# Dilated attention and convolution in an encoder layer: queries copied into the second pattern's order, loads moved ahead, the last heads regrouped

## The chip, the cores and the metric

The kernel runs on one core of a Trainium2 chip. The metric is the device time of one execution in microseconds. The engines are TensorE (PE; its weight loads are listed apart as PEld), VectorE (DVE), ScalarE (ACT), GpSimd (POOL) and SyncE (SP), which issues most of the DMAs. Each engine works through its own queue in order; where one needs another's result it waits on a semaphore.

## The reference

One layer of a bidirectional encoder over 2048 positions of width 1024, float32. An RMSNorm and one projection give queries, keys and values (8 heads of 64) and the two inputs of a gated convolution (512 channels). Then come attention and convolution side by side, an output projection, a cross-attention to 256 memory rows, an MLP of width 4096 with a squared ReLU, and a last RMSNorm. What the change touches is the attention over three dilated patterns, merged by their log-denominators, and the convolution:

```
DILATED_PATTERNS = ((128, 1), (512, 4), (2048, 16))
for window, d in DILATED_PATTERNS:
    half = window // (2 * d)
    o, lse = banded_attention(to_strided(q, d), to_strided(k, d), to_strided(v, d), half)
    outs.append(from_strided(o, d, B)); lses.append(from_strided(lse, d, B))
w = softmax(stack(lses), axis=0)
o = sum(w[..., None] * stack(outs), axis=0)
...
u = a * sigmoid(g)
u = conv1d_depthwise(u, conv_w, width=31) + conv_b
u = silu(layernorm(u, ln_g, ln_b))
```

Pattern 0 takes neighbouring positions, pattern 1 every fourth, pattern 2 (the far one) every sixteenth; each looks 64 steps to either side.

## The kernel before

Matrices are kept as a high and a low part, and a product is three matmuls (high by high, low by high, high by low; `mm3`, lines 198 to 200). Weights come as tiles `raw` of 512 KB, are split by ACT (high, line 189) and DVE or POOL (low, line 190), and have a few places each.

The positions are handled in four groups of 512. After the projections (0 to about 550 us of the profile) the attention of group 0 runs (`att(0, p2_)`), woven with the rest of the convolution gates (`rest`) and the first convolution's layer norm. Far units for all positions (`att_far`, line 800 and on) are done here, four per head, ahead of that head's near units. Then `post(p)` runs for each group: output projection (`o`), cross-attention (`xs`, `x`), MLP (`up`, `dn`), final norm. While `post(p)` runs, the attention and convolution of group p + 1 are woven in by rates: `weave` advances a side by so many steps per step of the main work. The order in which instructions stand on each engine is then fixed by the framework's scheduler when the program is built. `issue_after` (in `pinned` and `after`) holds some of them behind the last instruction of a named engine.

A near unit (`unit` in `att_units`) handles one head, one pattern and two blocks of 128 queries. It has three parts, taken in turn with those of the next units: scores on PE (`s`, line 948, four matmuls of 128x256: two blocks, each with the high and the low queries as weights), mask and row minimum on DVE (line 751) and the exponential on ACT (752); transposes on PE (758) and a split into `ph` and `pl` (761, 762); the product with the values on PE (`opt`, lines 766 to 768). Two units (g = 0, 1) make a head and pattern. Within a head pattern 1 comes first, then pattern 0. The weights of pattern 0's scores are 128 neighbouring columns of the query tile; those of pattern 1 are every fourth:

```
if pat == 0:
    qs = slice(P * blk, P * blk + P)
    kv = k[:, :, 8 * blk + 12:8 * blk + 28].rearrange("p r (c i) -> p c r i", c=2)
else:
    qs = slice(blk, 512, 4)
    kv = k[:, blk:16:4, 0:64].rearrange("p r (c i) -> p c r i", c=2)
```

Queries and keys are loaded on SP for a pair of heads at a time (`load_keys`): the high part `qh` (two transfers, two buffers), the low part `ql` (one transfer, one of two buffers) and, in groups 1 to 3, the near keys `k` of 512 KB (two buffers). In group 0 the near units use the far keys `k3`. The values of a pair are loaded together at the end of the pair before (`load_v`).

Pattern 1's and the far pattern's outputs go through memory (`oscr`, stored from ACT's queue), to come back in natural order. When a pair is done `combine` loads them (`ld`), forms the weights of the three patterns and adds them up on POOL (lines 868 to 894, `cat`), with small steps on DVE and ACT between, PE transposes the result (`catT`, line 902), and it goes to memory (`cath`, `catl`) for the output projection, which reads the last pair's part last.

The convolution of 512 positions and 128 channels (`conv_unit`) loads its input `cu` and does 31 steps on DVE (lines 210 and 212), then stores; four such units make a group.

POOL does little else after the projections: the power in `newton_rsqrt` (176), and one subtraction per tile in the convolution's norm (268).

Of the kernel before, what the change touches and what calls it, by code (L numbers as in the profile page):

```python
# [47 lines left out]
def hybrid_layer(ctx, tc, A, out):  # L48
# [157 lines left out]
    def conv_unit(c, n, alloc):  # L206
        u = alloc("u", (P, 542), f"cu{c}_{n}")
        dma(u, uscr[c][:, 512 * n:512 * n + 542])
        acc = alloc("acc", (P, 512), f"cacc{c}_{n}")
        DVE.tensor_scalar(acc, u[:, 0:512], cw[:, c, 0:1], gain("conv_b", c), op0=ALU.mult, op1=ALU.add)  # L210
        for t in range(1, CW):
            DVE.scalar_tensor_tensor(acc, u[:, t:t + 512], cw[:, c, t:t + 1], acc, op0=ALU.mult, op1=ALU.add)  # L212
            if t % 4 == 0:
                yield
        dma(cscr[c][:, 512 * n:512 * (n + 1)], acc)
        yield
# [502 lines left out]
    with ExitStack() as st:  # L719
        lbk = pool("lin_k", stack=st)  # L720
        cu = pool("conv0", stack=st)
        conv0 = pinned(conv_units(cu, 0, (0, 1)), "dve")
        weave(islice(steps, 31), (vsc, 0.42), (conv0, 0.5))
        drain(vsc, conv0)
        next(steps)
    with ExitStack() as st:
        lbv = pool("lin_v", stack=st)
        cu = pool("conv0b", stack=st)
        conv0 = pinned(conv_units(cu, 0, (2, 3)), "dve")
# [47 lines left out]
    def load_keys(h, p):  # L777

        k = None
        if p:  # L780
            k = kq.tile([P, 16, 64], F32R, tag="k", name=f"k{p}{h}", bufs=2)
            dma(f(k), f(kscr[:, :, h].rearrange("x d r i -> (x d) r i")[:, :, 32 * p:32 * p + 64]))
# [21 lines left out]
    def att_far(p2_, h, k, vt, q):  # L804
# [105 lines left out]
    def att_units(p, far, then):  # L910
# [4 lines left out]
        vt = {}  # L915

        def load_v(pr):
            es = slice(pr * 2 * VW, (pr + 1) * 2 * VW)
            if far:
                vt[2] = far.tile([P, 16, 2 * VW], F16, tag="v3", name=f"v3_{pr}")  # L920
                dma(vt[2], vtok[256:256 + S, es].rearrange("(i r) e -> i r e", r=16))
            vt[1] = aq.tile([P, 4, 2, 2 * VW], F16, tag="v2", name=f"v2_{p}{pr}")
            for c in range(2):
                src = vtok[512 * (p + c):512 * (p + c) + 512, es].rearrange("(i a b) e -> b a i e", a=4, b=4)
                for b in range(4):
                    dma(vt[1][:, b, c], src[b])
            vt[0] = aq.tile([P, 5, 2 * VW], F16, tag="v1", name=f"v1_{p}{pr}")
            for c in range(5):
                t0 = 256 + 512 * p + P * c - 64
                dma(vt[0][:, c], vtok[t0:t0 + P, es].rearrange("(i r) e -> r i e", r=16))  # L930

        def unit(pr, hh, pat, g, k, q_, os_, opt):
# [3 lines left out]
            for z in range(2):  # L936
# [5 lines left out]
                else:  # L942
                    qs = slice(blk, 512, 4)
# [28 lines left out]
            if g and hh and not pat:  # L972
                then(pr, os_)
                if pr < H // 2 - 1:
                    load_v(pr + 1)

        for pr in range(H // 2):
            if pr == 0:
                load_v(0)
            K = [load_keys(2 * pr + hh, p) for hh in range(2)]  # L980
            o0 = aq.tile([P, 4, 2, ROW], F32, tag="o0", name=f"o0_{p}{pr}", bufs=2)
            o1 = None
            for hh in range(2):
                k, q_ = K[hh]
                if far:
                    h, k = 2 * pr + hh, keys
# [3 lines left out]
                if hh == 0:  # L990
                    o1 = (far if far and pr % 2 else aq).tile([P, 4, 2, ROW], F32, tag="o1", name=f"o1_{p}{pr}")
# [53 lines left out]
    with ExitStack() as st:  # L1045
# [26 lines left out]
        weave(islice(first, 74), (rest, 0.8))  # L1072
# [302 lines left out]
```

## Time and profile before

| | |
|---|---|
| time, three runs | 2935.51, 2942.90, 2942.61 us; median 2942.61 |
| the profiled execution | 2945.54 us, its span 2943.7 us |
| PE busy | 2867.2 us (97%) |
| PEld (weight loads) | 2447.8 us (83%) |
| DVE busy | 1836.3 us (62%) |
| ACT busy | 1188.1 us (40%) |
| POOL busy | 396.8 us (13%) |
| moved by DMA | 434.87 MB |
| mean granted clock | 0.988 |

The span runs from the first to the last instruction; the time is a little longer. A row of the timeline gives start and length in microseconds, engine, line, operation, what is written from what, and in brackets the engine's idle time before it and what ended that. A row of the table by stages gives for each engine the busy time and the number of instructions, then the granted clock, the mean share of the DMA engines and GB/s. A row of a source line gives the number of instructions and the shortest, median and longest duration in ns. A row of waits gives the total, the number of times and the longest.

### The profile page before, as it was taken

To read this page: it belongs to the slowest core of one execution; us is meant where nothing else is said; L and a number is where in the kernel's file an instruction comes from. 1 tells how busy PE (TensorE), PEld (TensorE's weight loads), DVE (VectorE), ACT (ScalarE), POOL (GpSimd) and SP (SyncE) were. 2 spreads that over 40 slices of the span, in tenths; PEclk is the share of its full clock that TensorE was granted. 3 is DMA by queue.
4 is the path that set the end of the run, shared out by engine and by line. 5 is a ranking of instruction groups with operands and counts; after the bars stand their busy time and mean duration, and the time that the engine had idled before them with its cause. 6 is when DMAs were issued, how large, how long until landed. Compare 5 with 4: busy or idle time off the path is not lost.

```text
span 2943.7 us, 42766 instructions
## 1 busy us (share of the span) xinstructions
PE 2867.2 (97%) x16396; PEld 2447.8 (83%) x16396; DVE 1836.3 (62%) x3295; ACT 1188.1 (40%) x2002; POOL 396.8 (13%) x470
## 2 busy tenths in 40 slices
PE   8999999989799999999999999999999999999999
PEld 7878889878598888888888888898888888888888
DVE  5636444555668866576697766677867555544445
ACT  5632211566345333344443334444433344432333
POOL 1346421122100111010020012000110110000000
PEclk9999999999899999999999999999999999999999
DMA  8978844889724544464353445624434355233332
GB/s 265 295 165 212 194 135 134 197 224 253 186 81 137 141 124 125 129 183 163 107 136 122 127 129 167 188 102 130 131 118 122 104 161 170 92 94 100 93 100 72
DMA packets 620804, 434.87 MB, mean 148 GB/s; under 512 B 191333, under 2 KB 549785, under 8 KB 620600
## 3 DMA queue, kind: packets, MB, share of 16 engines
q1 hardware_dynamic: 582168, 414.05, 49.7%
q10 hardware_dynamic: 38432, 18.09, 2.5%
q8 instruction: 129, 2.11, 0.3%
q14 instruction: 75, 0.61, 0.1%
HBM read 340.42 MB, written 91.64 MB: 147 GB/s over the span
## 4 chain that ended last, share of the span: by engine, by line
PE 79%; DVE 3%; DMA 2%; ACT 2%; issue 1%; SPq 1%; POOL 1%; ACTq 0%; POOLq 0%; DVEq 0%
PE up L198 8%; PE dn L198 8%; PE up L200 8%; PE up L199 8%; PE dn L199 8%; PE dn L200 8%; PE s L948 2%; PE x L198 2%; PE xs L198 2%; PE x L200 2%; PE x L199 2%; PE o L198 2%; PE xs L200 2%; PE xs L199 2%; PE o L199 2%; PE o L200 2%
## 5 line engine op out<-in xcount | busy, mean ns | idle before, releaser
L199 PE MATMUL dn<-hhl,whi_d 128*128 128x512 f32 (+1 forms) x1056 | 404.2, 385 | 0.0
L200 PE MATMUL dn<-hhh,wlo_d 128*128 128x512 f32 (+1 forms) x1056 | 403.4, 384 | 0.0
L198 PE MATMUL up<-mh,whi_u 128*128 128x512 f32 x1024 | 402.0, 393 | 0.5 <-DVE rl L1246 0.5
L198 PE MATMUL dn<-hhh,whi_d 128*128 128x512 f32 (+1 forms) x1056 | 400.3, 392 | 1.7 <-DVE h L1264 1.6
L200 PE MATMUL up<-mh,wlo_u 128*128 128x512 f32 x1024 | 399.5, 390 | 0.0
L199 PE MATMUL up<-ml,whi_u 128*128 128x512 f32 x1024 | 398.8, 389 | 0.0
L212 DVE SCALAR_TENSOR_TENSOR cacc<-cu,cw,cacc 128x512 f32<-128x512 f32 x480 | 384.3, 803 | 5.3
L1264 DVE TENSOR_TENSOR h<-h,dn 128x512 f32<-128x512 f32 (+1 forms) x264 | 172.4, 667 | 216.6 <-PE dn L200 215.2
L189 ACT CAST whi_d<-raw_d 128x1024 fp32r<-128x1024 f32 x128 | 134.6, 1051 | 403.8 <-PE up L199 352.0
L189 ACT CAST whi_u<-raw_u 128x1024 fp32r<-128x1024 f32 x128 | 134.6, 1051 | 379.8 <-PE dn L199 322.5
L198 PEld LDWEIGHTS dn<-hhh,whi_d 128*128 128x128 f32 x1056 | 197.5, 188 | 40.9 <-DVE h L1264 5.4
L1246 DVE SCALAR_TENSOR_TENSOR rl<-up,ssumx 128x512 f32<-128x512 f32 x128 | 88.0, 691 | 229.4 <-PE up L200 225.6
L200 PEld LDWEIGHTS dn<-hhh,wlo_d 128*128 128x128 f32 x1056 | 198.5, 188 | 39.2
L199 PEld LDWEIGHTS dn<-hhl,whi_d 128*128 128x128 f32 x1056 | 198.8, 188 | 35.8
L200 PEld LDWEIGHTS up<-mh,wlo_u 128*128 128x128 f32 x1024 | 192.2, 188 | 40.3
L199 PEld LDWEIGHTS up<-ml,whi_u 128*128 128x128 f32 x1024 | 192.4, 188 | 38.2
L198 PEld LDWEIGHTS up<-mh,whi_u 128*128 128x128 f32 x1024 | 192.2, 188 | 38.5 <-DVE rl L1246 0.9
L752 ACT ACTIVATE sm<-sm,o 128x256 f32<-128x256 f32 (+1 forms) x384 | 159.0, 465 | 118.4 <-DVE o L751 109.6
L190 DVE TENSOR_TENSOR wlo_d<-raw_d,whi_d 128x1024 fp32r<-128x1024 f32 x128 | 158.2, 1236 | 24.6 <-ACT whi_d L189 24.6
L190 DVE TENSOR_TENSOR wlo_u<-raw_u,whi_u 128x1024 fp32r<-128x1024 f32 x128 | 158.9, 1242 | 22.3 <-ACT whi_u L189 22.1
L751 DVE CUSTOM_DVE_ANT_0 sm<-s,mask 128x256 f32<-128x256 f32 (+1 forms) x384 | 127.8, 374 | 47.7 <-PE s L948 33.4
L762 DVE TENSOR_TENSOR pl<-pt,ph 128x512 f16<-128x512 f32 x160 | 109.2, 686 | 66.6 <-ACT ph L761 66.6
(386 smaller groups left out, 6521.6 us busy)
## 6 DMA issues: line engine op xcount, KB each, us to landing
raw_u<-in_w_up_dram SPq DMA_DIRECT2D x128, 512.0 KB
raw_d<-in_w_down_dram SPq DMA_DIRECT2D x128, 512.0 KB
raw_o<-in_w_out_dram SPq DMA_DIRECT2D x32, 512.0 KB
raw_a<-ascr SPq DMA_DIRECT2D x32, 512.0 KB
raw_b<-bscr SPq DMA_DIRECT2D x32, 512.0 KB
v<-vtok SPq DMA_DIRECT2D x208, 65.0 KB
k<-kscr SPq DMA_DIRECT2D x24, 512.0 KB
k<-kscr SPq DMA_DIRECT2D x8, 1152.0 KB
```

Source lines behind the costliest of these rows:

```text
L189: ACT.copy(hi, raw)
L190: (lo_eng or DVE).tensor_tensor(lo, raw, f(hi), op=ALU.subtract)
L198: PE.matmul(o, lh, rh, start=first, stop=False)
L199: PE.matmul(o, lh, rl, start=False, stop=False)
L200: last["pe"] = PE.matmul(o, ll, rh, start=False, stop=end)
L212: DVE.scalar_tensor_tensor(acc, u[:, t:t + 512], cw[:, c, t:t + 1], acc, op0=ALU.mult, op1=ALU.add)
L751: last["dve"] = DVE.tensor_tensor_reduce(dst, so, mask[:, 256 * m:256 * m + nk], 1.0, 3e38, ALU.add, ALU.min, mn)
L752: last["act"] = ACT.activation(dst, dst, AF.Exp, bias=mn, scale=-1.0)
L762: DVE.tensor_tensor(pl, pt, ph, op=ALU.subtract)
L948: last["pe"] = PE.matmul(o, q_[x][:, qs], kv, start=x == 0, stop=x == 1)
L1246: last["dve"] = DVE.scalar_tensor_tensor(r, pt, 0.0, rsb, op0=ALU.max, op1=ALU.mult)
L1264: last["dve"] = DVE.tensor_tensor(hs[m][:, sl], hs[m][:, sl], pt, op=ALU.add)
```

## The change

Four things are done.

In the near attention pattern 0 now comes first and pattern 1 second. A new function `turned` copies a head's queries on POOL, high (128x512) and low (64x512), so that each block's every-fourth columns lie side by side; pattern 1's scores read the copy. The copy takes the second of the `qh` buffers and the second of the `ql` buffers, so that loaded queries have one buffer each. Queries and keys of a head are loaded one head ahead, behind the previous head's pattern-0 units, instead of for two heads at a time. Values are loaded in two parts, pattern 0's behind the last pattern-0 unit of a pair, the others behind its last unit.

In group 0 the last two heads (`end`) do the far units of both first, then pattern 1 of both, then pattern 0 of both, with the old reading of the queries; their near keys are loaded apart (`keys_of`) into the places of the far queries.

The convolution's input is loaded by a function of its own: two steps ahead of the first unit, and one unit ahead for the others (not in the two early pools).

The combination waits one step longer before its loads, except for the last pair of group 0, and the rates of three weaves are changed.

```diff
-    def conv_unit(c, n, alloc):
+    def conv_load(c, n, alloc):
         u = alloc("u", (P, 542), f"cu{c}_{n}")
         dma(u, uscr[c][:, 512 * n:512 * n + 542])
+        return u
+
+    def conv_unit(c, n, alloc, u):
...
-    def conv_units(pl, n, cs=range(4)):
-        for c in cs:
-            yield from conv_unit(c, n, lambda role, shape, name: pl.tile(list(shape), F32, tag=role, name=name, bufs=2))
+    def conv_units(pl, n, cs=(0, 1, 2, 3), ahead=True):
...
+        u = conv_load(cs[0], n, alloc)
+        yield
+        yield
+        for i, c in enumerate(cs):
+            nxt = conv_load(cs[i + 1], n, alloc) if ahead and i + 1 < len(cs) else None
+            yield from conv_unit(c, n, alloc, u)
+            u = nxt or (conv_load(cs[i + 1], n, alloc) if i + 1 < len(cs) else None)
...
-    def load_keys(h, p):
+    def load_keys(h, p, slot=0):
...
-        ql = qlow[h % 2]
+        ql = qlow[slot]
...
+    def turned(h, p, q):
+
+        qh = kq.tile([P, 512], F32R, tag="qh", name=f"qt{p}{h}", bufs=2)
+        for d, t in ((qh, q[0]), (qlow[1][0:64], q[1][0:64])):
+            POOL.tensor_copy(d.rearrange("p (b i) -> p b i", b=4), t.rearrange("p (i b) -> p b i", b=4))
+        return qh, qlow[1]
...
+            if h == H - 1 and rq > 1:
+                q[rq - 2] = keys_of(4 + rq, 0)
...
     def combine(p, pr, o0):
 
+        if p or pr < 3:
+            yield
...
-                    qs = slice(blk, 512, 4)
+                    qs = slice(P * blk, P * blk + P) if turn_ else slice(blk, 512, 4)
...
-            if g and hh and not pat:
-                then(pr, os_)
+            if g and hh:
+                if pat == lastpat:
+                    then(pr, o0)
                 if pr < H // 2 - 1:
-                    load_v(pr + 1)
+                    load_v(pr + 1, (1, 2) if pat else (0,))
...
+        load_v(0, (2, 0, 1))
+        nxt = load_keys(0, p)
         for pr in range(H // 2):
-            if pr == 0:
-                load_v(0)
-            K = [load_keys(2 * pr + hh, p) for hh in range(2)]
+            end = far and pr == H // 2 - 1
...
+                if end:
+                    two.append(q_)
+                    if hh == 0:
+                        nxt = load_keys(h + 1, p, 1)
+                    continue
+                qt = turned(h, p, q_)
+                yield from units(0, q_, hh, k)
+                if h < H - 1:
+                    nxt = load_keys(h + 1, p)
+                yield from units(1, qt, hh, k)
+            if end:
                 for pat in (1, 0):
-                    opt = []
-                    for g in range(2):
-                        yield unit(pr, hh, pat, g, k, q_, o1 if pat else o0, opt)
+                    for hh in range(2):
+                        yield from units(pat, two[hh], hh, q3[hh])
...
-        weave(islice(first, 74), (rest, 0.8))
+        weave(islice(first, 66), (rest, 0.86))
...
-            weave(islice(pinned(main, "pe"), 6), (first, 2.4))
+            weave(islice(pinned(main, "pe"), 6), (first, 3.4))
...
-        sides = [(att(p + 1), 0.95), (conv(cv, p + 1), 0.55)] if p + 1 < NG else []
+        sides = [(att(p + 1), 0.95), (conv(cv, p + 1), 0.6)] if p + 1 < NG else []
```

More of the change, by code (lines that the diff above doesn't have):

```diff
@@ L775, in low_parts, with keys_of @@
         return t
-    def load_keys(h, p):
+    def keys_of(h, p):
+        k = kq.tile([P, 16, 64], F32R, tag="k", name=f"k{p}{h}", bufs=2)
+        dma(f(k), f(kscr[:, :, h].rearrange("x d r i -> (x d) r i")[:, :, 32 * p:32 * p + 64]))
+        return k
+    def load_keys(h, p, slot=0):
         k = None
         if p:
-            k = kq.tile([P, 16, 64], F32R, tag="k", name=f"k{p}{h}", bufs=2)
-            dma(f(k), f(kscr[:, :, h].rearrange("x d r i -> (x d) r i")[:, :, 32 * p:32 * p + 64]))
+            k = keys_of(h, p)
         qh = kq.tile([P, 512], F32R, tag="qh", name=f"qh{p}{h}", bufs=2)
-        ql = qlow[h % 2]
+        ql = qlow[slot]
         cols = slice(512 * p, 512 * p + 512)
@@ L915, in att_units, with load_v, unit @@
         vt = {}
-        def load_v(pr):
+        o1 = [None]
+        def load_v(pr, pats):
             es = slice(pr * 2 * VW, (pr + 1) * 2 * VW)
-            if far:
+            if 2 in pats and far:
                 vt[2] = far.tile([P, 16, 2 * VW], F16, tag="v3", name=f"v3_{pr}")
                 dma(vt[2], vtok[256:256 + S, es].rearrange("(i r) e -> i r e", r=16))
[L922 to L932, printed above, removed]
+            if 0 in pats:
+                vt[0] = aq.tile([P, 5, 2 * VW], F16, tag="v1", name=f"v1_{p}{pr}")
+                for c in range(5):
+                    t0 = 256 + 512 * p + P * c - 64
+                    dma(vt[0][:, c], vtok[t0:t0 + P, es].rearrange("(i r) e -> r i e", r=16))
+            if 1 in pats:
+                vt[1] = aq.tile([P, 4, 2, 2 * VW], F16, tag="v2", name=f"v2_{p}{pr}")
+                for c in range(2):
+                    src = vtok[512 * (p + c):512 * (p + c) + 512, es].rearrange("(i a b) e -> b a i e", a=4, b=4)
+                    for b in range(4):
+                        dma(vt[1][:, b, c], src[b])
+        def unit(pr, hh, pat, g, k, q_, opt, turn_, lastpat, o0):
+            if pat and not g and not hh:
+                o1[0] = (aq if pr % 2 or not far else far).tile([P, 4, 2, ROW], F32, tag="o1", name=f"o1_{p}{pr}")
+            os_ = o1[0] if pat else o0
             sp_ = ps("S", "s")
@@ L989, in att_units, with units @@
                     yield from att_far(far, h, k, vt, q3)
-                if hh == 0:
-                    o1 = (far if far and pr % 2 else aq).tile([P, 4, 2, ROW], F32, tag="o1", name=f"o1_{p}{pr}")
+                def units(pat, q, hh, k):
+                    opt = []
+                    return [unit(pr, hh, pat, g, k, q, opt, not end, 0 if end else 1, o0) for g in range(2)]
+                if end:
[9 more added lines that the diff above has]
+            if end:
                 for pat in (1, 0):
-                    opt = []
-                    for g in range(2):
-                        yield unit(pr, hh, pat, g, k, q_, o1 if pat else o0, opt)
+                    for hh in range(2):
+                        yield from units(pat, two[hh], hh, q3[hh])
     def att(p, far=None):
```

13 lines of the change are left out of this document (8 added, 5 removed).

## The prediction

> **What bounds the kernel now.** I read the page's engine table first, then one table by stages, then single units of the attention on TensorE (PE), then the one stage in which PE stands still.
>
> ```profile
> span 2943.7 us, 42766 instructions
> PE 2867.2 (97%) x16396; PEld 2447.8 (83%) x16396; DVE 1836.3 (62%) x3295; ACT 1188.1 (40%) x2002; POOL 396.8 (13%) x470
> ```
>
> ```profile
> core 0: us, PE busy (x) PEld busy (x) DVE busy (x) ACT busy (x) POOL busy (x), PEclk, DMA share, GB/s
> 550.00:750.00 200.00, 184.96 (x1623) 160.72 (x1621) 114.96 (x467) 136.77 (x298) 37.53 (x57) 0.96 0.91 227
> 750.00:805.00 55.00, 37.39 (x200) 29.12 (x200) 36.38 (x63) 19.60 (x33) 10.44 (x16) 0.81 0.59 163
> 805.00:1400.00 595.00, 592.32 (x3363) 504.71 (x3363) 418.02 (x717) 244.00 (x391) 53.99 (x73) 1.00 0.46 136
> 1400.00:2010.00 610.00, 603.06 (x3439) 514.65 (x3439) 420.93 (x735) 249.62 (x411) 55.13 (x72) 0.99 0.46 134
> 2010.00:2550.00 540.00, 538.78 (x2939) 454.41 (x2938) 361.37 (x599) 217.53 (x341) 52.75 (x72) 1.00 0.43 130
> ```
>
> Three different stages show. From 805 us on, where the attention of position groups 1 to 3 is woven into the output projection and the MLP, PE is busy 592.3 of 595, 603.1 of 610 and 538.8 of 540 us: there nothing but PE work counts, and a microsecond taken from PE is a microsecond of the span. From 550 to 750 us (attention of group 0, with the last convolution gates between) PE is idle 15 of 200 us, so a saving is only partly paid out. From 750 to 805 us (group 0's last heads, the start of the output projection) it is idle 17.6 of 55 us and the granted clock is 0.81: there the chain of waits counts, not PE's work.
>
> Now the attention's scores. The first five rows are a pattern-1 unit (its four matmuls and what follows), the next five a pattern-0 unit; then one weight load of each of the two.
>
> ```profile
> 1105.85 0.28 PE L948 MATMUL s<-k,qh 128*128 128x256 f32 x1
> 1105.97 0.39 PE L948 MATMUL s<-k,ql 128*128 128x256 f32 x1
> 1106.20 0.41 PE L948 MATMUL s<-k,qh 128*128 128x256 f32 x1
> 1106.44 0.39 PE L948 MATMUL s<-k,ql 128*128 128x256 f32 x1
> 1106.67 0.39 PE L198 MATMUL dn<-hhh,whi_d 128*128 128x512 f32 x1
> ...
> 1131.37 0.29 PE L948 MATMUL s<-k,qh 128*128 128x256 f32 x1
> 1131.50 0.30 PE L948 MATMUL s<-k,ql 128*128 128x256 f32 x1
> 1131.63 0.30 PE L948 MATMUL s<-k,qh 128*128 128x256 f32 x1
> 1131.78 0.30 PE L948 MATMUL s<-k,ql 128*128 128x256 f32 x1
> 1131.91 0.40 PE L198 MATMUL up<-mh,whi_u 128*128 128x512 f32 x1
> ```
>
> ```profile
> 1106.07 0.33 PEld L948 LDWEIGHTS s<-k,qh 128*128 128x128 f32 x1
> ...
> 1131.50 0.19 PEld L948 LDWEIGHTS s<-k,qh 128*128 128x128 f32 x1
> ```
>
> Both units are four matmuls of 128x256. The pattern-1 unit holds PE for 1106.67 - 1105.85 = 0.82 us, the pattern-0 unit for 1131.91 - 1131.37 = 0.54 us, because the weight load, whose queries pattern 1 takes every fourth column, lasts 0.33 instead of 0.19 us and cannot hide behind a matmul of 256 columns.
>
> **Step 1, queries copied.** Pattern 1 now loads its weights from a copy in its own order, so its unit should cost what a pattern-0 unit costs.
>
> ```profile
> L948 PE MATMUL s<-k,ql 128*128 128x256 f32 x256 | 85.8, 344 | 0.0
> L948 PE MATMUL s<-k,qh 128*128 128x256 f32 x256 | 85.1, 342 | 2.1 <-ACT xp L1207 1.6 <-DVE o L751 0.5
> ```
>
> These are 512 matmuls, four in a unit: 128 units, 64 of them pattern 1. Group 0's last two heads keep the old reading (2 x 2 units), so 60 units change: 48 in groups 1 to 3, 12 in group 0. A unit saves 0.82 - 0.54 = 0.28 us at least; where the unit before is of the same kind its first load hides less, and another pattern-0 unit, at 744.97 us, takes 0.48.
>
> ```profile
> 744.97 0.28 PE L948 MATMUL s<-k,qh 128*128 128x256 f32 x1
> 745.45 0.20 PE L766 MATMUL opt<-v,ph 128*128 128x65 f16 x1
> ```
>
> That makes 0.34 us. Ends: 48 x 0.28 = 13.4 us (group 0 pays nothing out) and 60 x 0.34 = 20.4 us. I take 0.34 for the 48, 16.3 us, and half for the 12, 2 us: 18.3 us.
>
> A rule of the Trainium skill speaks against this step: the page "TensorE: Matmul & The Clock Gate", section "LDWEIGHTS (loading the stationary operand)", makes a load's time the column count over 1.2 per ns, and says that only the 128 columns matter. By it both patterns would load alike and the copy would buy nothing; the trace differs, with 0.33 against 0.19 us for the same 128 columns.
>
> What it costs: two POOL copies a head, for 30 heads (8 x 4 - 2). The nearest row is the copy that reorders far queries.
>
> ```profile
> L655 POOL COPY sth_q<-qh_q x12: 1073/1096/1536, 279.4 to 382.9; 128x512 f32<-128x512 f32 x12
> L655 POOL COPY stl_q<-ql_q x12: 1072/1415/1546, 290.1 to 383.8; 128x512 f32<-128x512 f32 x12
> ```
>
> Between 1.1 and 1.55 us each, 1.3 taken: 2.6 us a head, 60 x 1.3 = 78 us more on POOL, which is busy 397 of 2944. On PE's path it costs nothing while the copies are done before the first pattern-1 scores. In the changed program's order the pattern-0 units of a head, now first, stand between: 3.4 us of PE's work at the shortest (head 0 of group 1), 4.7 to 5.2 in group 0, 5 and more elsewhere, counted at 0.23 us for a matmul of 512 columns and 0.12 for one of 256. That is the cover; the third rival is its loss.
>
> The copies also press on VectorE (DVE), which reads SBUF beside POOL: three convolution steps with POOL nearly still, then four beside POOL's multiplications.
>
> ```profile
> 770.02 2.31 DVE L212 SCALAR_TENSOR_TENSOR cacc<-cu,cw,cacc 128x512 f32<-128x512 f32 x3
> 772.84 4.55 DVE L212 SCALAR_TENSOR_TENSOR cacc<-cu,cw,cacc 128x512 f32<-128x512 f32 x4
> ```
>
> 0.77 us becomes 1.14, so 78 us of copies stretch DVE by 78 x 0.37 / 1.14 = 25 us at most. DVE is idle 177 us between 805 and 1400 alone; hidden, at the worst 1 us in each of three groups, where the MLP begins.
>
> **Loads of queries, keys and values.** Each head's queries (three transfers) and keys (one) now go one head ahead, behind the previous head's pattern-0 scores. They wait on SP for PE, and the low halves for POOL too, since they have one buffer instead of two; behind them queue weight tiles. Those have room:
>
> ```profile
> ACT whi_d L189 <- PE up L199: 352.0, 108, 5.6
> SPq L57 <- DVE wlo_d L190: 455.0, 106, 8.0
> ```
>
> The split of a weight tile waits 352.0 / 108 = 3.3 us for PE to free its place, so a tile may land 3 us later unseen. The value loads keep their number and are split in two, each two units ahead of its use. Two key tiles of 512 KB are added for group 0's last heads. All together: 0, ends -1 and +4 us.
>
> **Steps 2 and 3, from 750 to 805 us.** In the order of what waits: the convolution's input, DVE, PE, then POOL's combination of the last pair and the projection matmul that needs it.
>
> ```profile
> 767.61 0.55 DVE L210 TENSOR_SCALAR cacc<-cu,cw,gv 128x512 f32<-128x512 f32 x1 [6.28 <-DMA cu<-uscr]
> 770.16 0.24 PE L768 MATMUL opt<-v,pl 128*128 128x65 f16 x1 [7.20 <-DVE pl L762]
> ...
> 773.00 1.39 POOL L888 TENSOR_TENSOR ce<-ce,csm 128x8 f32<-128x8 f32 x3 [0.32 <-DVE csm L885]
> 775.35 2.94 POOL L892 TENSOR_TENSOR ld<-ld,ce 128x512 f32<-128x512 f32 x2
> 778.25 3.21 POOL L894 TENSOR_TENSOR cat<-cat,ld 128x512 f32<-128x512 f32 x2
> 781.52 1.12 PE L902 MATMUL catT<-ident,cat 128*128 128x128 f32 x4 [1.54 <-POOL cat L894]
> 788.20 1.65 PE L198 MATMUL o<-cath,whi_o 128*128 128x512 f32 x3 [1.82 <-DMA cath<-cath]
> ```
>
> DVE stands 6.28 us for the convolution's input, and PE 7.20 us behind it. In the changed order that load is issued well ahead and its first use stands behind the last scores: 7.2 us go. What is late next is POOL's combination: 788.20 - 770.16 = 18.0 us from the last pair's last product to the projection matmul that needs it. Two things lengthen it. The copies for head 1 of group 1 stand before the combination's last two additions in POOL's new order, 2.6 us, and they wait for queries that SP issues only behind five value loads. And more projection matmuls are now spent before it: in the changed order 9 of 512 columns lie between the last product and the combination's transposes, where 18 lay before, so 9 x 0.23 = 2.1 us of cover is gone. Grouping the last heads' far units, and storing pattern 1 four units earlier, takes waits out ahead of the chain: at best the other idle before 770 us, about 3 us, of which I take 1. Sum: -7.2 + 2.6 + 2.1 - 1.0 = -3.5 us. Ends: -13 (the stall, those 3 us and 3 us of the low clock go, nothing is lengthened) and +5 (both lengthenings, and as long a wait elsewhere).
>
> **Sum.** -18.3 - 3.5 - 0 = -21.8 us, against the profiled execution's 2945.54 us (span 2943.7 and 1.8 around it): 2923.7. That execution is 2.9 above the median of 2942.61, so by the median 2920.8. I say 2921 us. For this kernel 0.3%, about 9 us, is the least that a measurement tells from no change.
>
> **The rivals.**
> First, the stage from 750 to 805 us gives all it can: -20.4 - 13 = -33 us, and with the rest of the low clock some -38: 2905 to 2909. For it speaks the 0.81 clock, against it POOL's 18.0 us chain, which stays. Chance 0.17.
> Second, the copy does not shorten the loads (the long load would be due to pattern 1 itself, not its stride): 2942.6 - 3.5 = 2939. Against it: the keys' moving side is the more broken one in pattern 0, which is the faster. The rule on columns above would give the same. Chance 0.05.
> Third, slower: PE's pattern-1 scores wait for the copies, since POOL works in order and a combination of some ten us can stand ahead. If each of 30 heads shows its 2.6 us, that is 78 us: 2942.6 - 21.8 + 78 = 2999. It decides from 21.8 / 30 = 0.7 us a head. Against it: in the changed order the combinations lie behind the copies of heads that PE needs first, or far ahead of them. Chance 0.09.
>
> **How the numbers follow.** Forecast 0.69 (its own range 2910 to 2936), first rival 0.17, second 0.05, third 0.09. Faster by over 0.3% takes the first rival and nearly all of the forecast, 0.82; within 0.3% the second and the forecast's upper end, 0.09; slower the third, 0.09. The range of 8 in 10 reaches from 2902 (first rival, with both ends of the loads) to 2938 (step 1 at its lower end, the transition at +5 and the loads at +4).
>
> **What would show it.** Right: the score matmuls of pattern 1 take 0.12 to 0.14 us start to start, all their weight loads 0.19 us but those of group 0's last heads; POOL some 475 us; no wait of PE on POOL's copies above 1 us; the wait of 7.2 us gone; PE's busy time from 805 us to the end some 16 us less. Wrong: score loads still at 0.33 us; waits of PE's scores on POOL; more than 18 us between the last pair's last product and the projection's last inputs; PE idle in the stages after 805 us.

## The result

The changed kernel takes 2957.74 us (median of 6 runs, 2953.18 to 2961.28), the kernel before 2940.36 us beside it (6 runs, 2931.78 to 2944.31). The ratio is 1.0062, with a 95% interval of 1.0043 to 1.0080: 0.6% slower, where 2921 us had been forecast. The profiled execution took 2954.55 us, 9.0 more than that of before.

The page of the changed kernel, with its span and engine table:

```profile
span 2952.8 us, 42973 instructions
PE 2844.3 (96%) x16396; PEld 2424.4 (82%) x16396; DVE 1849.7 (63%) x3295; ACT 1187.0 (40%) x2002; POOL 476.4 (16%) x530
```

PE is busy 22.9 us less (2867.2 before), and yet the span is 9.1 us longer. The table by stages says where; the rows are those of the prediction, with the third cut at 852 us, where the changed kernel's output projection of group 0 ends (826 before):

```profile
core 0: us, PE busy (x) PEld busy (x) DVE busy (x) ACT busy (x) POOL busy (x), PEclk, DMA share, GB/s
550.00:750.00 200.00, 161.94 (x1433) 138.01 (x1432) 99.12 (x424) 123.77 (x272) 43.73 (x64) 0.94 0.87 213
750.00:805.00 55.00, 38.68 (x305) 33.48 (x303) 28.14 (x75) 21.31 (x44) 15.86 (x24) 0.87 0.70 166
805.00:852.00 47.00, 41.51 (x212) 34.98 (x213) 31.33 (x42) 19.15 (x26) 1.82 (x2) 0.88 0.46 151
852.00:1400.00 548.00, 544.92 (x3070) 459.45 (x3069) 395.87 (x669) 226.52 (x363) 75.61 (x88) 1.00 0.48 140
1400.00:2010.00 610.00, 600.75 (x3520) 513.99 (x3518) 431.11 (x749) 250.17 (x411) 77.88 (x89) 0.99 0.44 131
2010.00:2550.00 540.00, 539.80 (x2986) 456.12 (x2985) 374.16 (x618) 222.78 (x353) 70.34 (x84) 1.00 0.45 135
```

From 852 us on PE is as full as it was. But from 550 to 750 us it is idle for 38 of 200 us (15 before), and from 750 to 852 us the granted clock is 0.87 and 0.88, where it was 1.00 from 805 us on before. The whole loss lies in the attention of group 0.

Two marks cut the program so that every kernel of this study can be compared: the first far score matmul of group 0, and the first matmul of the norm behind group 0's output projection. A row of a tile gives count, shortest, median and longest ns, and the first and last start. Before, then after:

```profile
L823 PE MATMUL s<-k,qh x128: 277/281/415, 538.3 to 733.0; 128*128 128x256 f32 x128
L1110 PE MATMUL nps<-ones,ssumo x32: 168/250/250, 825.8 to 2489.7; 128*128 128x1 f32 x32
```

```profile
L845 PE MATMUL s<-k,qh x128: 277/280/562, 530.9 to 747.1; 128*128 128x256 f32 x128
L1157 PE MATMUL nps<-ones,ssumo x32: 168/250/250, 852.5 to 2499.4; 128*128 128x1 f32 x32
```

Group 0 takes 852.5 - 530.9 = 321.6 us instead of 825.8 - 538.3 = 287.5, so 34.1 more. What follows takes 2952.8 - 852.5 = 2100.3 instead of 2943.7 - 825.8 = 2117.9, so 17.6 less. (The first mark lies between 530.9 and 538.3 in all executions, without visible relation to the edits; the changed kernel's profiled execution happened to be early, which hides 7.4 of the 34.1 in its span.)

The marks do not hold quite the same work. Between them stand 2030 matmuls in the kernel before and 2044 to 2046 in the changed kernel and all its variants: 15 more of the cross-attention's `xs` (128x256) stand ahead of the second mark. At 0.12 us from start to start that is 1.8 us which only changes sides, so some 32 us are lost and some 16 gained.

The timeline of PE in group 0 of the changed kernel shows its largest waits (idle time and what ended it in brackets); the row at 791.35, which has none, is one of the last pair's last product:

```profile
538.52 0.55 PE L845 MATMUL s<-k,qh 128*128 128x256 f32 x1 [5.37 <-DVE o L762]
...
732.15 0.55 PE L845 MATMUL s<-k,qh 128*128 128x256 f32 x1 [7.17 <-DVE o L762]
...
745.73 0.55 PE L845 MATMUL s<-k,qh 128*128 128x256 f32 x1 [4.55 <-DVE o L762]
...
789.29 0.79 PE L980 MATMUL s<-k,qh 128*128 128x256 f32 x2 [6.59 <-DMA qh<-qscr]
...
791.35 0.24 PE L779 MATMUL opt<-v,pl 128*128 128x65 f16 x1
...
806.95 1.11 PE L928 MATMUL catT<-ident,cat 128*128 128x128 f32 x4 [8.83 <-POOL cat L920]
...
813.74 1.65 PE L198 MATMUL o<-cath,whi_o 128*128 128x512 f32 x3 [0.86 <-DMA cath<-cath]
```

The five longest waits make 32.5 us together, of which the kernel before has only 1.5 (at its combination); its own 7.20 us behind the convolution's input is gone. All waits of PE between the marks add up to 65.2 us, and to 32.3 in the kernel before: these 32.9 us more are nearly the whole loss. The second and third of the five are for DVE's row minimum of the far units of heads 6 and 7, and DVE waits for a buffer whose store has not landed (4.61 us here, and 3.60 us at 745.07):

```profile
731.50 0.29 DVE L762 CUSTOM_DVE_ANT_0 sm<-s,mask 128x128 f32<-128x128 f32 x1 [4.61 <-DMA oscr<-o]
```

The far outputs (tile `o3`) have two buffers. In the old order a head's near units stand between two heads' far units, and the store lands behind them; back to back, it is waited for.

### The profile page after: what moved, and what is told of

Same layout as the page of the kernel before. It is cut to its first block, busy times and chain, and to the rows that moved or that the text cites. A ratio compares the mean times of both kernels' runs of the same rounds, so it can differ in the third digit from the quotient of the medians.

```text
span 2952.8 us, 42973 instructions
## 1 busy us (share of the span) xinstructions
PE 2844.3 (96%) x16396; PEld 2424.4 (82%) x16396; DVE 1849.7 (63%) x3295; ACT 1187.0 (40%) x2002; POOL 476.4 (16%) x530
## 4 chain that ended last, share of the span: by engine, by line
PE 73%; DMA 6%; DVE 3%; ACT 3%; SPq 2%; issue 1%; POOL 1%; ACTq 0%; POOLq 0%; DVEq 0%
PE dn L198 8%; PE dn L199 8%; PE dn L200 8%; PE up L198 7%; PE up L200 7%; PE up L199 7%; PE xs L198 2%; PE xs L199 2%; PE xs L200 2%; PE o L198 2%; PE o L199 2%; PE o L200 2%; SPq L57 2%; PE s L980 2%; PE pt L769 2%; PE x L198 2%
```

## The experiments

All are read by the two marks: group 0 is the first mark to the second, the rest is from there to the end of the span. The ratio is to the kernel before, run beside it.

| kernel | median us | ratio, 95% interval | group 0 | rest |
|---|---|---|---|---|
| before | 2940.36 | 1 | 287.5 | 2117.9 |
| before, second profile (e15) | | | 289.9 | 2118.6 |
| changed | 2957.74 | 1.0062 (1.0043 to 1.0080) | 321.6 | 2100.3 |
| e1, last pair not regrouped | 2952.24 | 1.0028 (1.0018 to 1.0038) | 321.5 | 2099.2 |
| e2, no copies | 2971.77 | 1.0084 (1.0069 to 1.0099) | 320.2 | 2114.9 |
| e3, neither | 2968.92 | 1.0082 (1.0066 to 1.0099) | 315.1 | 2115.9 |
| e4, old weave rates | 2954.57 | 1.0028 (1.0017 to 1.0038) | 314.8 | 2099.5 |
| e5, no empty steps | 2950.85 | 1.0020 (1.0011 to 1.0029) | 314.9 | 2102.3 |
| e6, later combinations | 2960.96 | 1.0056 (1.0040 to 1.0073) | 319.8 | 2100.8 |
| e7, last pair in the old order | 2949.31 | 1.0011 (1.0002 to 1.0021) | 308.1 | 2101.4 |
| e8, e5 + e6 + e7 | 2931.35 | 0.9951 (0.9936 to 0.9966) | 295.5 | 2100.5 |
| e9, copies in the old order | 2931.09 | 0.9960 (0.9947 to 0.9973) | 293.3 | 2101.5 |
| e10, e5 + e6 | 2949.33 | 1.0017 (1.0005 to 1.0030) | 311.5 | 2101.2 |
| e11, e5 + e7 | 2938.00 | 0.9976 (0.9961 to 0.9990) | 303.4 | 2100.9 |
| e12, third far buffer, no pads | 2978.85 | 1.0119 (1.0091 to 1.0146) | 317.1 | 2117.5 |
| e13, no pads | 2982.05 | 1.0121 (1.0100 to 1.0141) | 326.6 | 2118.9 |
| e14, e9 with copies made twice | 2947.85 | 1.0012 (1.0000 to 1.0023) | 297.7 | 2113.6 |

Ten runs of one kernel spread over some 8 to 12 us, so a profiled execution can lie several us off its median; the two columns on the right are of one execution each. The medians come from five groups of runs (changed; e1 to e4; e5 to e8; e9 to e12; e13 and e14), beside which the kernel before took 2940.36, 2943.96, 2945.18, 2944.85 and 2943.96 us: a difference of medians from two groups can be off by some 5 us, and by their ratios e1 to e14 lie some 3 to 8 us lower against the changed kernel than by their medians.

### Copies and regrouping, each undone (e1 to e4)

e1 puts the last pair of group 0 back between far and near units:

```diff
-            end = far and pr == H // 2 - 1
+            end = False
...
-        weave(islice(first, 66), (rest, 0.86))
+        weave(islice(first, 74), (rest, 0.8))
...
-            weave(islice(pinned(main, "pe"), 6), (first, 3.4))
+            weave(islice(pinned(main, "pe"), 6), (first, 2.4))
```

> The copies, the second pattern second and the loads ahead stay; only the last pair of group 0 goes back to the order far units, near units, far units, near units (with the weave's old rates, 74 at 0.8 and 2.4, which that order needs). Theory A (the regrouped end of group 0 is what lost the time, through the far outputs' two buffers, the late loads of group 1 and the combination that stands last): the 17.7 us gained in groups 1 to 3 stay and the 26.7 us lost by the end of group 0's projection go, so 2916 to 2924 us, some 2920, and the first norm matmul starts within 4 us of 825.8. Rival B (the copies on GpSimd, the combination behind them and the DVE beside them slow group 0 wherever the units stand): still 2945 us or more, the first norm matmul at 840 or later.

e2 keeps the regrouping and reads the queries with the old stride:

```diff
-                qt = turned(h, p, q_)
+                qt = q_
...
-        ql = qlow[slot]
+        ql = qlow[h % 2]
```

> The changed kernel without the copies: the second pattern's queries are read with the stride of four as before, all else (order, loads ahead, regrouped last pair, rates) stays. Theory A: the loss of group 0 stays (first norm matmul at 848 to 856) and groups 1 to 3 lose what contiguous columns gave, so 2957.7 + 17.7 = 2975 us, 2968 to 2980. Rival B: the loss of group 0 goes with the copies, so 2957.7 + 17.7 - 26.7 = 2949 us or less, and the first norm matmul at 835 or before.

e3 does both, e4 changes the two rates of e1 alone.

> Both undone: no copies (strided queries) and the last pair of group 0 in the old order with the old rates. What stays is the second pattern going second, the loads a unit ahead and the split loads of V. Theory A and B both: about the kernel before, 2930 to 2944 us; if the two parts add, this is the run with copies and old end (theory A: 2920) plus 17.7, so some 2938. Rival C (the reordering and the loads ahead have a price of their own): 2950 or more.

> The changed kernel with only the two weave rates put back (74 units at 0.8 and 2.4 in place of 66 at 0.86 and 3.4). Theory A (order of the units, not how densely they are woven): within 5 us of the changed kernel, 2953 to 2963. Rival D (the faster rate of 3.4 packs the last units beside too little other work and makes the waits): half of the 26.7 us or more goes, so 2945 us or less.

My first theory fell with e1: without the regrouping the kernel is still at 2952 us, and group 0 takes 321.5 us, as long as in the changed kernel (in e1's slowest run, 2960.44 us, which is the profiled one). And e3, with neither copies nor regrouping, is at 2969 and not at 2938: group 0 keeps 315.1 us. So much of the loss came with something that all four still have: the second pattern second, the combination a step later, or the loads. The copies themselves do what they were meant to: from e2 to the changed kernel the rest falls from 2114.9 to 2100.3, by 14.6 us, and from e3 to e1 by 16.7. The old rates (e4) give 3 us by the median and 6.8 in group 0.

The largest wait of e1 and of e3 is one row each, the last pair's combination (e1, then e3):

```profile
813.01 1.12 PE L925 MATMUL catT<-ident,cat 128*128 128x128 f32 x4 [17.07 <-POOL cat L917]
```

```profile
801.04 1.11 PE L925 MATMUL catT<-ident,cat 128*128 128x128 f32 x4 [20.36 <-POOL cat L917]
```

The second pattern's outputs go to the scratch and come back in the order of positions (`ld`) before the combination can start. With that pattern last, store, reload and combination stand bare at the end: 17 and 20 us where the kernel before waits 1.54. (As the profiled run of e1 was its slowest, 17 may be more than it usually waits.) The changed kernel's regrouping works as a remedy for this, and brings it to 8.83 us, but costs about as much in the waits shown above.

### Three prices (e5 to e8)

The diff of the convolution has two empty steps that stand in group 0 too, where no load goes ahead. e5 takes them out there:

```diff
         u = conv_load(cs[0], n, alloc)
-        yield
-        yield
+        if ahead:
+            yield
+            yield
```

> The changed kernel, but the two empty steps that the load ahead put in front of the convolution stand only where the load is really ahead, not in group 0. The four runs so far lost 5.8 to 7.8 us at group 0's first far unit (wait of 4.4 to 5.4 us on the row minimum behind the sum of the convolution's channels, whose last load stands on SP behind the loads of keys, queries and values; before it stands ahead of them, and with this edit it does again). Theory E (the loss of group 0 has three separate prices, and this order on SP is the first): the wait of 5.4 us at 532 is gone and the time falls by 5 to 8 us from the changed kernel's 2957.7, to 2950 to 2953. Rival F (group 0 is held by its DMA traffic, 0.97 to 0.99 busy before between 650 and 750, so whatever is gained early is waited for later): 2956 to 2959.

e6 puts the combinations of pairs 0 to 2 of group 0 two units later:

```diff
-            for _ in range(2 if pr < 3 else 1):
+            for _ in range(4 if pr < 3 else 1):
```

> The changed kernel, but in group 0 the combination of pairs 0 to 2 begins two units later. Theory E: the second price is the combination's first minimum, which now stands in DVE's order before its reload from the scratch has landed, because the second pattern's outputs are stored last (waits of PE of 4.2 us near 612 and 2.6 + 3.5 us at 668 to 692 in the changed kernel, 2.6 and none before). With two more units between, the time falls by 4 to 9 us, to 2949 to 2954. Rival F (DMA traffic holds the stretch): 2956 to 2959. Rival G (a later combination pushes its product and the store of the joined heads into the next pair's far units): 2960 or more.

e7 is e1 with the last pair in the order of the kernel before, second pattern first, with strided queries; e8 has all three edits.

```diff
+                if end:
+                    if hh == 0:
+                        nxt = load_keys(h + 1, p, 1)
+                    yield from units(1, q_, hh, k)
+                    yield from units(0, q_, hh, k)
+                    continue
```

> The run with copies and the last pair in the old place (e1, 2952.2 us), and in that pair alone the second pattern first, with strided queries, as in the kernel before. e1 waits 17.1 us on the last pair's combination, since the second pattern's outputs are stored last and come back only then (20.4 us in the strided run, 8.8 us in the changed kernel, 1.7 us before). Theory E: the third price is this wait at the end of group 0; it shrinks to 5 us or less, and the time falls by 10 to 16 us to 2936 to 2942. Rival F: another wait takes its place in the same stretch, 2948 to 2953.

> The three edits together: no empty steps in group 0, combinations of pairs 0 to 2 two units later, last pair in the old order; copies, loads ahead and second pattern second elsewhere. Theory E, if the prices add: from e1's 2952.2 less 5 to 8, less 4 to 9, less 10 to 16, so 2919 to 2933, some 2926, 0.6% under the kernel before; the first norm matmul at 826 to 834. Rival F: not under 2938.

Theory E is right on e5: 2950.9 us, and group 0 is shorter by 6.7 us. The SP queue of before, of the changed kernel and of e5, near the first far unit:

```profile
518.69 0.32 SPq L57 DMA_DIRECT2D cscr<-cacc  x1
...
520.89 0.32 SPq L57 DMA_DIRECT2D lc<-cscr  x1
521.31 1.24 SPq L57 DMA_DIRECT2D k<-kscr  x1
```

```profile
517.68 0.32 SPq L57 DMA_DIRECT2D cscr<-cacc  x1
518.09 0.39 SPq L57 DMA_DIRECT2D k<-kscr  x1
...
530.77 0.58 SPq L57 DMA_DIRECT2D lc<-cscr  x1
```

```profile
516.18 0.32 SPq L57 DMA_DIRECT2D cscr<-cacc  x1
...
518.40 0.32 SPq L57 DMA_DIRECT2D lc<-cscr  x1
```

The two steps moved the convolution's last store to a later place in the program, so that its reload `lc` stands behind group 0's first keys, queries and values: it is issued 13.1 us after the store, where the kernel before and e5 need 2.2. DVE's sum of the channels waits for it, and stands ahead of the row minima (changed kernel):

```profile
537.26 0.69 DVE L240 TENSOR_TENSOR lsum<-lsum,lc 128x512 f32<-128x512 f32 x1 [5.02 <-DMA lc<-cscr]
```

That is PE's wait of 5.37 us at 538.5, and e5 no longer has it.

e6 alone gave nothing: 2961.0 us is where rival G put it, though e11 below speaks against G's reason, that a later combination is itself a burden. e7 alone gave little by the median, as its rival F had it (2949.3 against e1's 2952.2, though 13.4 us of group 0 in the profiled executions). Together with e5 they gave 26 us: e8 is at 2931.4, 0.5% under the kernel before. The prices do not simply add: a part of what one edit frees is taken by the next wait on the same stretch.

### What is left of each (e9 to e11)

> The changed kernel with its regrouped end, without the empty steps in group 0 and with the combinations of pairs 0 to 2 two units later: the run with all three edits (e8, 2931.4 us) with the changed kernel's end of group 0 in place of the old one. Theory: the regrouped far units with two output buffers and the queries of group 1 behind its loads of values keep their waits (7.2 + 4.6 + 3 to 7 us), so 2943 to 2951. Rival J (in e8 it was the later combination and the steps that won, not the old end): 2930 to 2936.

> The run with the three edits (e8, 2931.4 us) without the later combinations: tells how the 18 us between e7 (2949.3) and e8 divide. If the steps are worth what they are in the regrouped kernel (some 7 to 10 us), 2939 to 2942, and the later combination the other 8 to 11, although alone, in the regrouped kernel, it gave nothing (2961.0). If the later combination is worth nothing here either, 2929 to 2934.

e10 and e8 differ in the end of group 0 alone (with the rates that belong to each): 2949.3 against 2931.4 us, and 311.5 against 295.5 in group 0. The regrouped end, with its rates, costs 16 to 18 us. From 700 us on, PE's waits of over 3 us are 8.27 and 5.68 us (the two row minima), 6.19 (group 1's queries) and 6.14 (the combination) in e10, 26.3 together; in e8 they are 4.18, 4.58 and, at the combination, 4.78, so 13.5. e11 and e8 differ in the later combinations alone: 2938.0 against 2931.4, and 303.4 against 295.5. That is the third price, and its row stands in DVE's order (e11, then PE's wait behind it):

```profile
668.20 0.17 DVE L891 TENSOR_TENSOR csm<-ld 128x8 f32<-128x8 f32 x1 [7.04 <-DMA ld<-oscr]
...
669.03 0.24 PE L780 MATMUL opt<-v,pl 128*128 128x65 f16 x1 [6.04 <-DVE pl L774]
```

DVE works in order, so a 0.17 us minimum that waits for its reload holds up the subtraction that PE needs; in e8, two units later, the reload has landed, and the same minimum at 668.18 us waits for nothing.

e9 asks the question directly: copies, but every pair in the order of the kernel before, second pattern first. The copy's buffer takes the next head's queries once the second pattern's scores are done, and the copy is made behind the first pattern's:

```diff
+        qt = turned(0, p, nxt[1], 1)
...
-                qt = turned(h, p, q_)
-                yield from units(0, q_, hh, k)
-                if h < H - 1:
-                    nxt = load_keys(h + 1, p)
-                yield from units(1, qt, hh, k)
+                yield from units(1, qt, hh, k)
+                if h < H - 1:
+                    nxt = load_keys(h + 1, p, (h + 1) % 2)
+                yield from units(0, q_, hh, k)
+                if h < H - 1:
+                    qt = turned(h + 1, p, nxt[1], h % 2)
```

> The copies in the kernel before's order: every pair, the last one too, has its second pattern first, with the copied queries, and the first pattern second; the next head's queries are loaded into the copy's buffer after the second pattern's scores and copied after the first pattern's. Last pair not regrouped, combination at once as before, no empty steps in group 0; loads ahead in groups 1 to 3 stay. Theory H (the turned queries are worth their 17 us, and nearly all that group 0 lost comes of putting the second pattern second, which stores its outputs last): 17.4 us under the kernel before from groups 1 to 3, up to 7 more from the convolution's wait near 770 and up to 4 from group 0's 16 turned units, so 2918 to 2928 us, and the wait of PE on the joined heads at the end of group 0 under 3 us. Rival B (the copies, on GpSimd ahead of the combination and beside DVE, slow group 0 by themselves): 2935 to 2946.

It takes 2931.1 us, 0.4% under the kernel before and 26.7 us under the changed one; the sign is theory H's, the size is 3 us outside its bounds, and the wait at the combination is 4.94 us where it said under 3. Its marks and its combination:

```profile
L846 PE MATMUL s<-k,qh x128: 277/280/415, 531.6 to 730.0; 128*128 128x256 f32 x128
L1156 PE MATMUL nps<-ones,ssumo x32: 168/250/250, 824.9 to 2473.1; 128*128 128x1 f32 x32
```

```profile
778.57 1.11 PE L925 MATMUL catT<-ident,cat 128*128 128x128 f32 x4 [4.94 <-POOL cat L917]
```

The rest has the full gain (2101.5), group 0 none: 293.3 us. So the second pattern's new place was no condition of the copies. e9 undoes that place, the regrouped end that answers it and the empty steps together, and with them 28.3 of the 34.1 us go, 6.7 of which are the steps' by e5. e8 keeps the second pattern second in pairs 0 to 2 and takes the same time, so there a later combination makes up for the new place.

### The third buffer, the pads, and the copies' own price (e12 to e15)

> The changed kernel with three buffers for the far outputs in place of two (three unused pads taken out to make room), nothing else. Theory: the two waits of PE behind the row minimum of heads 6 and 7's far units (7.2 and 4.6 us), which stand for a buffer whose store has not landed, shrink to 3 us or less together, and the time falls by 5 to 11 us from 2957.7, to 2947 to 2953. Rival F: heads 6 and 7's loads or the combination that follows wait for as long as the stores did, 2955 to 2960.

> The changed kernel without its three unused pads, two far output buffers as before: the control for e12 (2978.9 us), whose trace shows every 512-column matmul from the first norm to the end at a median of 231 ns start to start, against 227 in the changed kernel. If the pads (where the operands lie) set this, 2957.7 + 17 = 2975 us, 2970 to 2983, and 231 ns again. If the third buffer is at fault in some other way, 2953 to 2962 and 227 ns.

```diff
-                o8[0] = p2_.tile([P, 8, ROW], F32, tag="o3", name=f"o3_{h}{rq}", bufs=2)
+                o8[0] = p2_.tile([P, 8, ROW], F32, tag="o3", name=f"o3_{h}{rq}", bufs=3)
...
-        p2_.tile([P, 176], F32, name="farpad")
...
-    wk.tile([P, 144], F32, name="wpad")
...
-    top.tile([P, 296], F32, name="tpad")
```

e12 was 21 us slower than the changed kernel, and e13, the pads alone, 24: the pads did it (below). Against its control e13 the third buffer gains 3 us by the medians, 9.5 in group 0. The two waits on the store are gone, and the next one stands in their place (PE in e12):

```profile
742.42 0.77 PE L843 MATMUL s<-k,qh 128*128 128x256 f32 x2 [7.65 <-DMA qh<-qfar]
```

The far queries have two buffers as well. So rival F was nearer the truth: with more buffers for the outputs, a good part of the time goes to the next load.

> The kernel of e9 (copies in the order of the kernel before, 2931.1 us) with each copy made twice, so 78 us more on GpSimd (some 554 us in all). The prediction's step that the copies hide beside other work: within 4 us of e9, 2927 to 2935. Rival B (copies on GpSimd cost by themselves): each 78 us of copies costs what group 0 is short of, 5 us or more, 2936 or more.

> The kernel before once more, for a second profiled execution. In the first its attention began at 538.3 us (first far score matmul) and took 287.5 us to the first norm matmul; the changed kernels began between 531 and 538 and took 293 to 322. If the start is chance and the stretch the kernel's own, it takes 285 to 290 us here whenever it begins; if a late start shortens the stretch (the transfers are then further ahead), an early start near 531 goes with some 293.

```diff
             POOL.tensor_copy(d.rearrange("p (b i) -> p b i", b=4), t.rearrange("p (i b) -> p b i", b=4))
+            POOL.tensor_copy(d.rearrange("p (b i) -> p b i", b=4), t.rearrange("p (i b) -> p b i", b=4))
```

A second set of copies costs 16.8 us (2947.9 against 2931.1), 4.4 in group 0 and 12.1 in the rest, so a second set is not hidden. Whether the first one is was not tried by itself; with it the rest gains 14.6 to 16.7 us, where step 1 forecast 16.3 without a cost. The convolution's steps on DVE, from 830 to 2920 us, in the changed kernel, in e9 and in e14:

```profile
L215 DVE SCALAR_TENSOR_TENSOR cacc<-cu,cw,cacc 128x512 f32<-128x512 f32 x356 | 276.8, 777 | 3.1
```

```profile
L215 DVE SCALAR_TENSOR_TENSOR cacc<-cu,cw,cacc 128x512 f32<-128x512 f32 x348 | 275.7, 792 | 3.1
```

```profile
L215 DVE SCALAR_TENSOR_TENSOR cacc<-cu,cw,cacc 128x512 f32<-128x512 f32 x348 | 287.0, 825 | 3.0
```

The mean grows from 777 and 792 to 825 ns. The Trainium skill ("SBUF — State Buffer", section "Who interferes with whom") says that a DVE instruction with two SBUF inputs contends with a GpSimd instruction that reads SBUF; the three rows agree with it. How the stretched steps turn into 12 us on PE, or whether the second copy's own 2.5 us a head do, was not separated.

e15 profiled the kernel before a second time: 289.9 us from a first mark at 537.3, about as late as the first time. An execution that started near 531 did not come up, so whether a late start shortens the stretch stays open. Of the 3.4 to 5.8 us by which e9's group 0 is longer than that of the kernel before, 1.8 are the matmuls that changed sides; the others stay open.

## Why the prediction was wrong

- **Step 1, queries copied: right in groups 1 to 3, wrong in group 0.** 16.3 us were forecast there; the rest fell by 17.6, of which the copies are 14.6 to 16.7 (e2 and e3 against their copied twins). The 2 to 3 us by which e2 and e3 are below the kernel before without copies are for the most part the 1.8 us that changed sides. The weight loads are as forecast (the copied queries in the changed kernel, then both patterns' in e2, which reads with the stride; shortest, median and longest ns):

```profile
L980 PEld LDWEIGHTS s<-k,qt x120: 186/188/330, 554.5 to 2324.6; 128*128 128x128 f32 x120
```

```profile
L980 PEld LDWEIGHTS s<-k,qh x256: 186/308/337, 552.9 to 2342.2; 128*128 128x128 f32 x128
```

  So the second rival, and the rule that only columns count, are out. The Trainium skill ("SBUF — State Buffer", section "Specifications (TRN2)") says that full bandwidth needs two accesses to each 16-byte line; every fourth float32 lies on a line of its own, so it would fit, but no run here tries another stride. The 2 us for group 0's 12 units did not come: in the profiled executions group 0 is 1.4 and 6.4 us longer with copies than without (the 6.4 between e1's slowest and e3's fastest run), and by the medians of these two, run side by side, the gain is 16.7 us, all of it that of the rest.
- **The copies' cover: right for what was made.** POOL is at 476.4 us (475 forecast), and PE waits for no copy over 1 us. But the margin I gave it (25 us on DVE, hidden) does not reach for twice as many copies, as e14 shows.
- **Loads, 0 us: wrong in place.** The price I looked for was late weight tiles in groups 1 to 3, and there is none. It was paid at the seam: the second half of group 1's first queries stands on SP behind eight value loads, and PE waits 6.59 us for it.

```profile
774.50 8.02 SPq L57 DMA_DIRECT2D v<-vtok  x8
...
783.38 0.78 SPq L57 DMA_DIRECT2D qh<-qscr  x1
```

  The wait goes with the end of group 0 as much as with the loads: it is 6.19 us in e10 and does not occur in e8 and e9, where the same lines load these queries.
- **The convolution, -7.2 us: right in the row, wrong in the sum.** The wait is gone. But I read "not in the two early pools" as no change there, and did not cost the two empty steps, which shift the convolution against SP's order: 6.7 us of group 0 (e5).
- **"Grouping the last heads' far units, and storing pattern 1 four units earlier, takes waits out": this is the step that failed.** I took a gain of 1 us for it. Measured, that end costs 16 to 18 us (e10 against e8, of which its rates may be 3 to 7, by e4), through the two output buffers, the queries above and the combination. The two output buffers alone are not all of it: e12's third one gave 3 us by the median.
- **The combination's two lengthenings, 2.6 + 2.1 us: right.** The last matmul of the last pair's last product starts at 791.85 in the changed kernel, and ACT copies the result at 792.12. From its first `pl` row to the projection were 788.20 - 770.16 = 18.0 us before; they are 813.74 - 791.35 = 22.4 now, 4.4 more where 4.7 were charged. Nine projection matmuls stand between the product and the transposes, as I counted, and the copies stand on POOL ahead of the last two additions (`cat`, from 804.47):

```profile
801.48 1.53 POOL L810 CAST qt<-qh 128x512 fp32r<-128x512 f32 x1
802.97 1.54 POOL L810 CAST ql<-ql 64x512 fp32r<-64x512 f32 x1
```

  So the sign of being wrong that I had put here, more than 18 us, did come.
- **What the sum had no term for.** Putting pattern 1 second moves the store of its outputs to the end of each pair, and with it the reload and the combination's first minimum. In pairs 0 to 2 that costs 3 to 8 us (e5 to e10, e11 to e8), and in the last pair it makes waits of 17 to 20 us (e1, e3), for which the regrouping can be read as a remedy. I had treated the order of the two patterns as free, costing only the cover of the copies.

The range's lower end, 2902, does not come out of the terms named for it: 2942.6 - 38 - 1 is 2904. Nothing hangs on it.

In the profiled executions, the 34.1 us of group 0 divide along one path of single edits as 6.7 (empty steps, changed to e5), 3.4 (combinations, to e10), 16.0 (end, to e8), 2.2 (second pattern first again in pairs 0 to 2, its combination at once, to e9), and 5.8 left (e9 to before), 1.8 of them work that changed sides. Another path would divide them otherwise, since the edits do not add.

## What to carry to other kernels

When two parts of a loop change places, follow each output as well as each input: the part that now comes last is the one whose store, reload and consumers have nothing left to hide behind. Two empty steps in a generator are an edit like any other, if a queue's order is made from them. And where a stretch has several waits in a row, removing one shows little by itself; judge the edits together before one is called useless (e6 gave nothing alone and 7 us in company).

## What the hardware showed beside this

The changed kernel, like the kernel before, has three unused pads of 704, 576 and 1184 bytes a partition. Without them the matmuls are slower: the last 300 us of the MLP hold fewer of them at a full clock (changed kernel, then e13):

```profile
2620.00:2920.00 300.00, 300.00 (x1333) 247.59 (x1332) 141.37 (x166) 90.25 (x111) 0.00 (x0) 1.00 0.32 95
```

```profile
2620.00:2920.00 300.00, 299.51 (x1304) 242.51 (x1303) 138.73 (x167) 89.50 (x112) 1.01 (x1) 1.00 0.32 95
```

That is 300 / 1333 = 225 ns a matmul against 299.51 / 1304 = 230, with nothing waiting, and 18.6 us over the rest of the kernel (2118.9 against 2100.3). Before 530 us, too, matmuls of 512 columns follow each other at a median of 232 ns, where the changed kernel and the kernel before have 227; so this is no part of what the change did. The pads hold nothing, so what their absence changes is where other tiles lie in SBUF, and that is the likely cause of these 2% of a matmul; which pad does it, and by what, was not tried.
